# Two DMA queues for the first loads, a first split on VectorE and another order of the first products in a one-core decoder-layer kernel

## Chip, core and metric

The kernel runs on one NeuronCore of one Trainium2 chip. The metric is device microseconds of one execution; a kernel's time is the median over its runs. The engines are called as in the profile: PE (TensorE matmul), PEld (its weight loads), DVE (VectorE), ACT (ScalarE), POOL (GpSimd) and SP (SyncE, which here only issues DMAs).

## What is computed

One decoder layer over 256 tokens of width 1024, all in float32. The change lies in its very first part, the input projection, so this is what matters of the reference:

```python
xn = rms_norm(x, attn_norm_g[l])          # x * rsqrt(mean(x*x) + eps) * g
proj = xn @ w_in[l]                       # 1024 x 3600: mq mk mv gq gk gv gr gate
...
x = x + concat[y_moba, y_gla] @ w_out[l]
x = x + (silu(h_gate) * h_val) @ w_ffn_down[l]
return rms_norm(x, final_norm_g)
```

## The kernel before

**Products in two parts.** Every float32 product a·b is made of three fp32r products: each operand is split into a high part (an fp32r copy) and a low part (the rest), and hi·hi, hi·lo and lo·hi are summed in PSUM (`mm3`, lines 109 to 111). The high part of a weight piece is an ACT activation (`Slot.split_hi`, line 92), the low part a DVE subtraction (`split_lo`, line 95). The input x is split in the same way by `xsplit(k)`: ACT multiplies the tile by the norm's gain and rounds (`ah`, line 169), DVE makes the rest (`al`, line 170). The RMS factor itself is applied later, on the projections' outputs.

**Tiles.** x lies transposed as `xg`: 8 columns of gains and 8 tiles of 128x256 (k = 0 to 7, over the 1024 inputs). The weights come in slots, through a ring of 4 raw buffers and 3 pairs of split buffers. The first four slots hold the group G (gq, the 16 gate columns and gk: 528 columns), two k-tiles to a slot; slot s has `in_wG` of k = 2s and 2s+1. The next ten hold the five other groups of 512 columns (`in_w`), half a group each.

**Order of the work.** PE's order is written out by hand: 64 steps q, in each of which `emit(q)` first does what `plan` holds for q, then the products of that step. Steps 0 to 7 are G's k = 0 to 7 (12 products each: two token halves, columns 0 to 272 into an `acc` bank and 272 to 528 into an `att` bank, three products each). Step 8 begins with `xnorm`: two tiny matmuls of `s1`, the sum over k of x squared, with a column of ones (line 248), before the products of the next group. What makes `s1` is `xsq` (ACT, line 234, two tiles at a time), three `xadd` (DVE, line 237) and `xsum` (DVE, line 241). The order on ACT and DVE is left to a scheduler, which lays it out from its own estimate of times.

**The start.** SP issues all DMAs, in the order of the code: x's tile 0, the first 272 columns of slot 0, the next 256, x's tile 1, the other half of slot 0, x's tile 2, half of slot 1, x's tile 3, the other half, and from there pairs of x tiles and whole slots (lines 147 to 166). ACT loads its function table first (line 54). Six small matmuls of zeros (`warm`, line 73) keep PE at work meanwhile.

Of the kernel before, what the change touches and what calls it, by code (L numbers as in the profile page):

```python
# [9 lines left out]
F32 = mybir.dt.float32  # L10
# [7 lines left out]
KT = 8  # L18
# [8 lines left out]
NG = 256 + RANK + 256  # L27
# [7 lines left out]
def trunk_kernel(ctx: ExitStack, tc: tile.TileContext, xT_d, wG_d, w5_d, wo_d, up_d, dn_d,  # L35
                 par_d, gla_g_d, fin_g_d, wgu_d, cos_d, sin_d, causal_d, lvl_d, ident_d, out_d):
    nc = tc.nc
    V, A, T, DMA = nc.vector, nc.scalar, nc.tensor, nc.sync
# [3 lines left out]
    ring = ctx.enter_context(tc.tile_pool(name="ring", bufs=1))  # L42
# [4 lines left out]
    def acc():  # L47
        return ps_acc.tile([128, 512], F32, name="acc")

    def att():  # L50
        return ps_att.tile([128, 512], F32, name="att")


    A.preload_act_table_set("natural_log_exp_and_others")
    par = const.tile([128, NPAR], F32, name="par")
    cos = const.tile([128, S], F32, name="cos")
    sin = const.tile([128, S], F32, name="sin")
# [18 lines left out]
    RAW, SPL = 4, 3  # L76
# [31 lines left out]
    def mm3(out, sh, sl, mh, ml, first, last, **kw):  # L108
        T.matmul(out, sh, mh, start=first, stop=False, **kw)  # L109
        T.matmul(out, sh, ml, start=False, stop=False, **kw)  # L110
        T.matmul(out, sl, mh, start=False, stop=last, **kw)  # L111

    slots = []
# [16 lines left out]
    nload = [0]  # L130

    def load_next():
        if nload[0] < len(items):
            items[nload[0]].load()
            nload[0] += 1


    xg = main.tile([128, KT + KT * S], F32, name="xg")
    pag = xg[:, :KT]
    xT = xg[:, KT:].rearrange("p (k t) -> p k t", k=KT)  # L140
    ah = main.tile([128, KT, S], F32R, name="ah", tag="ah")
    al = main.tile([128, KT, S], F32R, name="al", tag="al")
# [2 lines left out]
    rsx = main.tile([128, 8], F32, name="rsx")  # L145

    slots[0].raw = ring.tile([128, 2048], F32, name="raw", bufs=RAW)
    def load_x(k0, k1):
        a, b = (KT + S * k0 if k0 else 0), KT + S * k1
        DMA.dma_start(xg[:, a:b], xT_d[:, a:b])  # L150

    load_x(0, 1)
    for a, b in ((0, 272), (272, NG), (NG, 2 * NG)):
        DMA.dma_start(slots[0].raw[:, a:b], slots[0].src[:, a:b])
        if b == NG:
            load_x(1, 2)
    nload[0] = 1
    load_x(2, 3)
    slots[1].raw = ring.tile([128, 2048], F32, name="raw", bufs=RAW)
    DMA.dma_start(slots[1].raw[:, :NG], slots[1].src[:, :NG])  # L160
    load_x(3, 4)
    DMA.dma_start(slots[1].raw[:, NG:2 * NG], slots[1].src[:, NG:])
    nload[0] = 2
    for s in range(2, 4):
        load_x(2 * s, 2 * s + 2)
        load_next()

    def xsplit(k):
        A.activation(ah[:, k], xT[:, k], AF.Copy, scale=pag[:, k:k + 1])
        V.scalar_tensor_tensor(al[:, k], xT[:, k], pag[:, k:k + 1], ah[:, k],  # L170
                               op0=ALU.mult, op1=ALU.subtract)
# [59 lines left out]
    st = {}  # L231
# [305 lines left out]
    def on(q, f, *a):  # L537
        plan.setdefault(q, []).append((f, a))

    for k in range(1, KT):  # L540
        on(k - 1, xsplit, k)
    for dst, src, q in ((ident, ident_d, 1), (par, par_d, 3), (wgu, wgu_d, 4), (cos, cos_d, 4),
                        (sin, sin_d, 4), (lvl, lvl_d, 10), (causal, causal_d, 14), (glag, gla_g_d, 24)):
# [20 lines left out]
    for l in range(7):  # L564
        b = 21 + 11 * l // 4
# [13 lines left out]
    for h in range(HM):  # L579
        b = 30 + 3 * h // 2  # L580
# [13 lines left out]
    for n, sl in enumerate(slots[1:], 1):  # L594
# [5 lines left out]
        on(qa, sl.split, 0, sl.n // 2)  # L600
        on(qa + (3 if q0 - qa > 4 else 1), sl.split, sl.n // 2, sl.n)

    slots[0].alloc()
    xsplit(0)
    for a, b in ((0, 272), (272, NG), (NG, 2 * NG)):
        slots[0].split(a, b)

    def emit(q):
        for f, a in plan.get(q, []):
            f(*a)  # L610

    names = ["G", "q", "k", "v", "gv", "r"]
    for q in range(48):
        g, k = divmod(q, 8)
        emit(q)
        if k == 0:
            if g == 0:
                st["G"] = [(acc(), att()) for _ in range(2)]
            else:
                st[names[g]] = [acc() for _ in range(2)]  # L620
        if g == 0:
            h_, l_ = slots[k // 2].view(NG)
            kk = k % 2
        else:
            h_, l_ = slots[4 + 2 * (g - 1) + k // 4].view(512)
            kk = k % 4
        if g in (1, 2):
            for pr in range(4):
                cs = slice(pr * 128, pr * 128 + 128)
                mm3(st[names[g]][pr // 2][:, (pr % 2) * S:(pr % 2 + 1) * S], h_[:, kk, cs], l_[:, kk, cs],  # L630
                    ah[:, k], al[:, k], k == 0 and pr % 2 == 0, k == KT - 1, skip_group_check=True)
            continue
        for tt in range(2):
            sh = ah[:, k, tt * 128:(tt + 1) * 128]
            sl = al[:, k, tt * 128:(tt + 1) * 128]
            if g == 0:
                a, b = st["G"][tt]
                parts = ((a[:, :272], 0, 272), (b[:, :256], 272, 528))
            else:
                parts = ((st[names[g]][tt], 0, 512),)  # L640
            for o, c0, c1 in parts:
                mm3(o, sh, sl, h_[:, kk, c0:c1], l_[:, kk, c0:c1], k == 0, k == KT - 1)
# [6 lines left out]
    for q in range(48, 64):  # L649
# [5 lines left out]
        h_, l_ = slots[14 + 2 * ph + j // 4].view(512)  # L655
        cs = slice((j % 4) * 128, (j % 4 + 1) * 128)
        for kk in range(4):
            k = 4 * ph + kk
# [281 lines left out]
    for tt in range(2):  # L940
        y = yy[:, tt]
        c = 12 * tt
# [87 lines left out]
```

## Time and profile before

| | before |
|---|---|
| median of 3 runs | 317.51 us (316.83 to 317.53) |
| the profiled execution | 317.25 us, of it a span of 315.4 us from first to last instruction |
| PE, DVE, ACT busy | 97%, 80%, 65% of the span |
| DMA, in slices of 7.9 us | 184, 385, 414, 413, 202 GB/s, then between 0 and 418 |
| granted TensorE clock over the span | 0.999 of full speed |

The busy share of PE counts a modelled end of each matmul, so a stretch that reads as all busy has no long gap, but is not PE at its peak. A row of the timeline gives start, duration, engine, line, what is written and read, the count of instructions that were merged, and in brackets the idle time of the engine before it with what ended it. Instructions of one engine overlap by a little, so the step from one start to the next is the price of one in a row of them.

### The profile page before, as it was taken

Reading aid. Unit: us, or ns where it says so; the run is one execution under the profiler, and the core shown is the slowest. Engines: PE = TensorE matmul, PEld = TensorE weight load, DVE = VectorE, ACT = ScalarE, POOL = GpSimd, SP = SyncE. Lnnn points to the kernel's source line nnn. Section 1 sums busy time; section 2 is a strip of 40 time slices with the busy share of each in tenths; the row PEclk is TensorE's granted clock in tenths of the full one; section 3 lists DMA queues with packets and bytes.
Section 4 is the critical chain, followed back from the end, with each engine's and each line's share of the span. In section 5 each row is a group of like instructions: output and inputs, shape, how many; then the busy total and the mean of one; then the engine's idle time right before and its main releaser. Section 6 shows DMA issues by size and latency. Waiting matters only on the chain.

```text
span 315.4 us, 5842 instructions
## 1 busy us (share of the span) xinstructions
PE 305.8 (97%) x2296; PEld 282.5 (90%) x2296; DVE 253.5 (80%) x478; ACT 203.7 (65%) x370; POOL 3.9 (1%) x17
## 2 busy tenths in 40 slices
PE   6999999999999999999999999999999999999992
PEld 5899997776888999999999999999999999999982
DVE  3987999999647577999999978887777777776653
ACT  5978989497858478366776555666665555534353
POOL 4000000000000000000000000000000000000000
PEclk9999999999999999999999999999999999999999
DMA  6999533342360515595555664454555722120003
GB/s 184 385 414 413 202 135 133 133 151 118 135 232 37 189 79 199 165 418 221 199 202 204 232 220 176 182 197 193 201 202 199 264 70 69 66 69 0 2 0 134
DMA packets 12300, 55.39 MB, mean 176 GB/s; under 512 B 1377, under 2 KB 2929, under 8 KB 7921
## 3 DMA queue, kind: packets, MB, share of 16 engines
q1 hardware_dynamic: 12272, 55.02, 47.3%
q8 instruction: 18, 0.29, 0.4%
q14 instruction: 10, 0.07, 0.1%
HBM read 53.97 MB, written 1.05 MB: 174 GB/s over the span
## 4 chain that ended last, share of the span: by engine, by line
PE 79%; DVE 10%; ACT 5%; issue 2%; DMA 2%; SPq 1%; DVEq 0%; ACTq 0%
PE att L110 14%; PE att L111 14%; PE att L109 14%; PE acc L110 11%; PE acc L109 10%; PE acc L111 10%; DVE lo L95 2%; DMA xg<-in_xT 2%; ACT qs L466 1%; DVE qt L351 1%; DVE att L495 1%; PE att L527 1%; DVE ATd L377 1%; DVE kt L345 1%; PE att L515 1%
## 5 line engine op out<-in xcount | busy, mean ns | idle before, releaser
L92 ACT ACTIVATE hi<-raw 128x1024 fp32r<-128x1024 f32 (+3 forms) x84 | 80.1, 971 | 51.0 <-PE att L110 43.2
L95 DVE TENSOR_TENSOR lo<-raw,hi 128x1024 fp32r<-128x1024 f32 (+3 forms) x86 | 93.6, 1098 | 13.5 <-ACT hi L92 13.4
L109 PE MATMUL att<-hh,hi 128*128 128x256 f32 x352 | 98.5, 280 | 0.0
L111 PE MATMUL att<-hh,lo 128*128 128x256 f32 x352 | 98.4, 279 | 0.0
L110 PE MATMUL att<-hl,hi 128*128 128x256 f32 x352 | 98.3, 279 | 0.0
L109 PEld LDWEIGHTS att<-hh,hi 128*128 128x128 f32 x352 | 66.2, 188 | 0.0
L111 PEld LDWEIGHTS att<-hh,lo 128*128 128x128 f32 x352 | 66.2, 188 | 0.0
L110 PEld LDWEIGHTS att<-hl,hi 128*128 128x128 f32 x352 | 66.2, 188 | 0.0
L757 DVE SCALAR_TENSOR_TENSOR c<-us,par,c 128x256 f32<-128x256 f32 x88 | 40.7, 482 | 4.1 <-ACT c L749 2.5
L749 ACT ACTIVATE c<-us,par 128x256 f32<-128x256 f32 x44 | 24.0, 591 | 21.5 <-DVE us L739 16.1
L111 PE MATMUL acc<-dhi,gl 128*128 128x512 f32 (+1 forms) x88 | 32.3, 367 | 0.0
L110 PE MATMUL acc<-dlo,gh 128*128 128x512 f32 (+1 forms) x88 | 32.2, 366 | 0.0
L109 PE MATMUL acc<-dhi,gh 128*128 128x512 f32 (+1 forms) x88 | 31.8, 361 | 0.0
L696 DVE TENSOR_TENSOR dlo<-draw,dhi 128x1024 fp32r<-128x1024 f32 x22 | 26.6, 1219 | 0.0
L739 DVE TENSOR_TENSOR us<-att,rb 128x512 f32<-128x512 f32 x20 | 13.8, 689 | 15.9 <-PE att L111 15.9
L109 PE MATMUL acc<-hi,ah 128*128 128x512 f32 (+1 forms) x64 | 25.2, 394 | 1.2 <-ACT hi L92 1.2
L110 PE MATMUL acc<-lo,ah 128*128 128x512 f32 (+1 forms) x64 | 24.1, 376 | 0.8 <-DVE lo L95 0.8
L111 PE MATMUL acc<-hi,al 128*128 128x512 f32 (+1 forms) x64 | 23.6, 368 | 0.0
L691 ACT ACTIVATE dhi<-draw 128x1024 fp32r<-128x1024 f32 x22 | 23.1, 1049 | 0.0
L110 PEld LDWEIGHTS acc<-dlo,gh 128*128 128x128 f32 x88 | 16.5, 188 | 3.0
L109 PEld LDWEIGHTS acc<-dhi,gh 128*128 128x128 f32 x88 | 16.6, 188 | 2.9
L111 PEld LDWEIGHTS acc<-dhi,gl 128*128 128x128 f32 x88 | 16.5, 188 | 2.6
(192 smaller groups left out, 528.6 us busy)
## 6 DMA issues: line engine op xcount, KB each, us to landing
raw<-in_up SPq DMA_DIRECT2D x22, 1024.0 KB, 4.8
draw<-in_dn SPq DMA_DIRECT2D x22, 512.0 KB, 5.7
raw<-in_w SPq DMA_DIRECT2D x8, 1024.0 KB, 7.3
raw<-in_wo SPq DMA_DIRECT2D x4, 1024.0 KB, 4.8
raw<-in_w SPq DMA_DIRECT2D x4, 512.0 KB, 7.2
raw<-in_wG SPq DMA_DIRECT2D x2, 528.0 KB, 7.0
out_y<-yy SPq DMA_DIRECT2D x4, 256.0 KB, 2.2
raw<-in_wG SPq DMA_DIRECT2D x3, 264.0 KB, 4.7
```

What stands on the lines that cost most here:

```text
L92: A.activation(self.hi[:, a:b], self.raw[:, a:b], AF.Copy)
L95: V.tensor_sub(self.lo[:, a:b], self.raw[:, a:b], self.hi[:, a:b])
L109: T.matmul(out, sh, mh, start=first, stop=False, **kw)
L110: T.matmul(out, sh, ml, start=False, stop=False, **kw)
L111: T.matmul(out, sl, mh, start=False, stop=last, **kw)
L345: V.tensor_mul(blk(kt)[:, :, 0, :], blk(gk_)[:, :, 0, :], blk(e)[:, :, 0, :])
L351: V.tensor_mul(o, q_, e_)
L691: A.activation(hi, downs[i][0], AF.Copy)
L696: V.tensor_sub(lo, d, hi)
L739: V.tensor_tensor(u[:, :, 2:], upo[i][2].rearrange("p (a t) -> p a t", a=2), rb[:, None, :].to_broadcast([128, 2, S]), op=ALU.mult)
L749: A.activation(cv[i][:, a], u[:, a, 2:], AF.Identity, bias=par[:, P_CB + m:P_CB + m + 1], scale=par[:, P_CW + 2 * 2 * NP + m:P_CW + 2 * 2 ...
L757: V.scalar_tensor_tensor(c[:, a], u[:, a, w:w + S], par[:, wc:wc + 1], c[:, a], op0=ALU.mult, op1=ALU.add)
```

## The change

Four things are done at the start of the program.

- x's tiles 0, 1 and 2 with 3 are now three DMAs on ACT's own queue, ahead of ACT's table load; SP's queue begins with slot 0's three pieces. Slot 1 is now one DMA of 1056 columns in place of two halves, and x's tiles 4 to 7 come between the later slots as before.
- The high part of slot 0's first 272 columns is a DVE copy in place of an ACT activation.
- The splits of slot 0 and of x's tiles 0 and 1 are written in another order (`xsplit(1)` now stands ahead of the plan).
- Step 0's twelve products no longer go through `mm3`: they run as hi·ah and hi·al of the first columns, hi·ah and hi·al of the others, then both lo·ah.

```diff
-    A.preload_act_table_set("natural_log_exp_and_others")
...
-    def load_x(k0, k1):
+    def load_x(q, k0, k1):
...
-        DMA.dma_start(xg[:, a:b], xT_d[:, a:b])
-
-    load_x(0, 1)
+        q.dma_start(xg[:, a:b], xT_d[:, a:b])
...
+    with tc.manual_schedule(engines={mybir.EngineType.Activation}):
+        load_x(A, 0, 1)
+        load_x(A, 1, 2)
+        load_x(A, 2, 4)
+        A.preload_act_table_set("natural_log_exp_and_others")
     for a, b in ((0, 272), (272, NG), (NG, 2 * NG)):
         DMA.dma_start(slots[0].raw[:, a:b], slots[0].src[:, a:b])
-        if b == NG:
-            load_x(1, 2)
     nload[0] = 1
-    load_x(2, 3)
-    slots[1].raw = ring.tile([128, 2048], F32, name="raw", bufs=RAW)
-    DMA.dma_start(slots[1].raw[:, :NG], slots[1].src[:, :NG])
-    load_x(3, 4)
-    DMA.dma_start(slots[1].raw[:, NG:2 * NG], slots[1].src[:, NG:])
-    nload[0] = 2
-    for s in range(2, 4):
-        load_x(2 * s, 2 * s + 2)
-        load_next()
+    load_next()
+    load_x(DMA, 4, 6)
+    load_next()
+    load_x(DMA, 6, 8)
+    load_next()
...
-    for k in range(1, KT):
+    for k in range(2, KT):
         on(k - 1, xsplit, k)
...
     slots[0].alloc()
+    V.tensor_copy(slots[0].hi[:, :272], slots[0].raw[:, :272])
     xsplit(0)
-    for a, b in ((0, 272), (272, NG), (NG, 2 * NG)):
-        slots[0].split(a, b)
+    slots[0].split_hi(272, NG)
+    slots[0].split_lo(0, 272)
+    slots[0].split_lo(272, NG)
+    xsplit(1)
+    slots[0].split(NG, 2 * NG)
...
+        if q == 0:
+
+            for mov, sta, c in ((h_, ah, 0), (h_, al, 0), (h_, ah, 1), (h_, al, 1), (l_, ah, 0), (l_, ah, 1)):
+                c0, c1 = ((0, 272), (272, 528))[c]
+                for tt in range(2):
+                    T.matmul(st["G"][tt][c][:, :c1 - c0], sta[:, 0, tt * 128:(tt + 1) * 128], mov[:, 0, c0:c1],
+                             start=mov is h_ and sta is ah, stop=False)
             continue
```

The scheduler lays out ACT and DVE anew, which moves instructions beyond those that the diff names. On DVE, from the first piece of slot 1 (`lo` of 128x528, needed by step 2) to what follows the sum of squares `s`, the order before was:

```order
L95 TENSOR_TENSOR lo<-raw,hi 128x528
L170 SCALAR_TENSOR_TENSOR al<-xg,ah 128x256
L237 TENSOR_TENSOR xsqs<-xsqs 128x512
L95 TENSOR_TENSOR lo<-raw,hi 128x528
L170 SCALAR_TENSOR_TENSOR al<-xg,ah 128x256 x2
L237 TENSOR_TENSOR xsqs<-xsqs 128x512
L95 TENSOR_TENSOR lo<-raw,hi 128x528 x2
L170 SCALAR_TENSOR_TENSOR al<-xg,ah 128x256 x2
L237 TENSOR_TENSOR xsqs<-xsqs 128x512
L95 TENSOR_TENSOR lo<-raw,hi 128x528 x2
L241 TENSOR_TENSOR s_325<-xsqs 128x256
L95 TENSOR_TENSOR lo<-raw,hi 128x1024
```

And the same stretch in the changed kernel, with two lines less in the numbers of the lines:

```order
L94 TENSOR_TENSOR lo<-raw,hi 128x528 x2
L168 SCALAR_TENSOR_TENSOR al<-xg,ah 128x256 x2
L235 TENSOR_TENSOR xsqs<-xsqs 128x512
L94 TENSOR_TENSOR lo<-raw,hi 128x528 x2
L168 SCALAR_TENSOR_TENSOR al<-xg,ah 128x256 x2
L235 TENSOR_TENSOR xsqs<-xsqs 128x512
L94 TENSOR_TENSOR lo<-raw,hi 128x528 x2
L168 SCALAR_TENSOR_TENSOR al<-xg,ah 128x256
L94 TENSOR_TENSOR lo<-raw,hi 128x1024
L235 TENSOR_TENSOR xsqs<-xsqs 128x512
L94 TENSOR_TENSOR lo<-raw,hi 128x1024
L239 TENSOR_TENSOR s_326<-xsqs 128x256
```

The sum `s`, which stood ahead of both 128x1024 pieces (the halves of the first `in_w` slot), now stands behind them, and so does the last addition of squares behind the first of them.

At the head of ACT's order, from the table load to the first piece of slot 1, there stood before:

```order
L54 ACT_TABLE_LOAD
L169 ACTIVATE ah<-xg 128x256
L92 ACTIVATE hi<-raw 128x272
L92 ACTIVATE hi<-raw 128x256
L169 ACTIVATE ah<-xg 128x256
L234 ACTIVATE xsqs<-xg 128x512
L92 ACTIVATE hi<-raw 128x528
L169 ACTIVATE ah<-xg 128x256
L92 ACTIVATE hi<-raw 128x528
```

and now there stands:

```order
L149 DMA xg<-in_xT 128x264
L149 DMA xg<-in_xT 128x256
L149 DMA xg<-in_xT 128x512
L156 ACT_TABLE_LOAD
L167 ACTIVATE ah<-xg 128x256
L91 ACTIVATE hi<-raw 128x256
L167 ACTIVATE ah<-xg 128x256
L91 ACTIVATE hi<-raw 128x528
L167 ACTIVATE ah<-xg 128x256
L232 ACTIVATE xsqs<-xg 128x512
L91 ACTIVATE hi<-raw 128x528 x2
```

Three DMA issues come ahead of the table load, one split has left for DVE, and the first squares moved behind the half of slot 0 and x's tile 2, just ahead of slot 1's two pieces.

## Rows read from the trace of the kernel before

**Rows 1.** The page: busy time by engine, and the chain that ended last.
```profile
PE 305.8 (97%) x2296; PEld 282.5 (90%) x2296; DVE 253.5 (80%) x478; ACT 203.7 (65%) x370; POOL 3.9 (1%) x17
...
PE 79%; DVE 10%; ACT 5%; issue 2%; DMA 2%; SPq 1%; DVEq 0%; ACTq 0%
```

**Rows 2.** The waits of PE, whole span: us in total, times, longest us.
```profile
PE acc L109 <- ACT hi L92: 1.2, 2, 0.9
...
PE acc L110 <- DVE lo L95: 0.8, 3, 0.4
PE att L527 <- ACT pe L500: 0.6, 1, 0.6
```

**Rows 3.** Timeline of PE: first product, two of one row of them, the sum's matmuls.
```profile
4.32 0.39 PE L109 MATMUL acc<-hi,ah 128*128 128x272 f32 x1 [0.35 <-ACT hi L92]
...
13.69 0.29 PE L111 MATMUL acc<-hi,al 128*128 128x272 f32 x1
...
15.51 0.28 PE L111 MATMUL att<-hi,al 128*128 128x256 f32 x1
...
19.28 0.50 PE L248 MATMUL att<-ones,s 128*128 128x1 f32 x4
```

**Rows 4.** Timeline of ACT to its first piece of slot 1.
```profile
0.73 1.28 ACT L54 ACT_TABLE_LOAD   x1 [0.73 <-PEq L1019]
3.44 0.51 ACT L169 ACTIVATE ah<-xg 128x256 fp32r<-128x256 f32 x1 [1.43 <-DMA xg<-in_xT]
...
6.13 0.61 ACT L234 ACTIVATE xsqs<-xg 128x512 f32<-128x512 f32 x1
6.65 0.63 ACT L92 ACTIVATE hi<-raw 128x528 fp32r<-128x528 f32 x1
7.18 0.49 ACT L169 ACTIVATE ah<-xg 128x256 fp32r<-128x256 f32 x1
8.26 0.65 ACT L92 ACTIVATE hi<-raw 128x528 fp32r<-128x528 f32 x1 [0.58 <-DMA raw<-in_wG]
```

**Rows 5.** Timeline of SP: its first DMA issues.
```profile
0.73 0.37 SPq L150 DMA_DIRECT2D xg<-in_xT  x1
1.16 0.89 SPq L154 DMA_DIRECT2D raw<-in_wG  x2
2.10 0.43 SPq L150 DMA_DIRECT2D xg<-in_xT  x1
```

**Rows 6.** Windows: busy us of PE, PEld, DVE, ACT, POOL; PEclk; DMA share, GB/s.
```profile
0.00:2.00 2.00, 0.95 (x4) 0.95 (x5) 0.17 (x1) 1.27 (x1) 1.47 (x10) 1.00 0.10 20
2.00:4.00 2.00, 1.97 (x10) 1.68 (x8) 0.02 (x1) 0.57 (x3) 1.94 (x5) 1.00 0.89 226
4.00:6.00 2.00, 1.52 (x10) 1.31 (x11) 1.16 (x3) 0.86 (x3) 0.35 (x1) 1.00 0.88 274
6.00:8.00 2.00, 0.86 (x5) 0.45 (x4) 1.17 (x3) 1.68 (x4) 0.00 (x0) 1.00 0.87 214
8.00:10.00 2.00, 1.93 (x14) 1.81 (x15) 1.48 (x4) 1.63 (x4) 0.00 (x0) 1.00 0.96 321
...
12.00:14.00 2.00, 1.71 (x14) 1.50 (x13) 2.00 (x5) 2.00 (x6) 0.00 (x0) 1.00 1.01 415
```

**Rows 7.** Timeline of DVE, from slot 1's first low part on.
```profile
8.94 0.71 DVE L95 TENSOR_TENSOR lo<-raw,hi 128x528 fp32r<-128x528 f32 x1 [0.52 <-ACT hi L92]
...
12.70 1.32 DVE L95 TENSOR_TENSOR lo<-raw,hi 128x528 fp32r<-128x528 f32 x2
13.94 0.87 DVE L170 SCALAR_TENSOR_TENSOR al<-xg,ah 128x256 fp32r<-128x256 f32 x2
14.73 0.68 DVE L237 TENSOR_TENSOR xsqs<-xsqs 128x512 f32<-128x512 f32 x1
15.34 1.32 DVE L95 TENSOR_TENSOR lo<-raw,hi 128x528 fp32r<-128x528 f32 x2
16.57 0.42 DVE L241 TENSOR_TENSOR s<-xsqs 128x256 f32<-128x256 f32 x1
16.91 1.22 DVE L95 TENSOR_TENSOR lo<-raw,hi 128x1024 fp32r<-128x1024 f32 x1
18.05 0.21 DVE L286 TENSOR_TENSOR id<-ident 128x64 f32<-128x64 f32 x1
```

More of the change, by code (lines that the diff above doesn't have):

```diff
@@ L631, in trunk_kernel @@
                     ah[:, k], al[:, k], k == 0 and pr % 2 == 0, k == KT - 1, skip_group_check=True)
+            continue
+        if q == 0:
[4 more added lines that the diff above has]
+                             start=mov is h_ and sta is ah, stop=False)
             continue
```

## The prediction

> **What bounds the kernel now.** I read the page first: PE is busy for 97% of the span and carries 79% of the chain that ended last [rows 1]. A kernel like this gets faster only where PE stands still, so the second view is PE's waits [rows 2]: 1.2 us for high parts, 0.8 us for low parts, both in the first steps, and one wait of 0.6 us in the attention (line 527). The start is therefore the place to look, and the timeline of PE [rows 3] gives its frame: first product at 4.32, and line 248, the first work behind group G, at 19.28. Without waits the 96 products of G would take 96 x 0.121 = 11.6 us, where 0.121 is (15.51 - 13.69) / 15 starts in an undisturbed piece of it [rows 3]. They took 15.0, so 3.3 us are lost between 4.32 and 19.28, and behind that PE loses almost nothing. Whatever the change gives must show as an earlier line 248, and later waits may eat it.
>
> Who is late there? ACT's timeline [rows 4] shows two kinds of idle time: for x's tiles and for slot 1's first half, which landed just before 8.26. The windows [rows 6] show the DMA engines 0.87 to 0.89 busy from 2 to 8 us but moving only 214 to 274 GB/s, against 415 later. From 8.94 on it is DVE that has no gap: each of its rows begins where the last one stepped off, up to the sum of squares `s` at 16.57 [rows 7], and 12:14 reads 2.00 of 2.00 [rows 6].
>
> **The change part by part.** I count from the profiled execution (317.25 us, 0.26 under the median of 317.51) and add the difference to the median.
>
> *The first step.* SP starts one DMA every 0.47 us (0.73, 1.16, the third at 2.10 behind two merged ones) [rows 5]. With two queues x's tile 0 and slot 0's first piece start together at 0.73. ACT now issues three DMAs first, by SP's price 3 x 0.43 = 1.3 us, so its table load (1.28 us, [rows 4]) ends at 3.3 instead of 2.0; the first tile of x was there at 3.44. That hides it, by little. The DVE copy of 272 columns has no row of its own; it lies between 0.21 (128x64) and 0.71 (128x528) [rows 7], and I take 0.4, as it is nearer in size to half a 128x528. First product at about 4.1. DVE makes lo ahead of al, so the order hi·al before lo cannot be met quite as written; still the twelve products are over by 6.0. Step 1 needs the second half of slot 0, which (below) is not split before 6.9. So the copy, the new order of products and the earlier first product are all worth nothing by themselves: the next step is late next, and if an ACT issue cost twice SP's, this too would be covered.
>
> *The loads up to slot 1.* Before, slot 1's first half landed at 8.24, with 132 + 136 + 128 + 128 + 264 + 128 + 264 = 1180 KB of 1024 bytes up to it in SP's queue, 1.21 MB. By the windows [rows 6] 2 x (20 + 226 + 274 + 214) = 1468 thousand bytes had moved by 8.0 and 1545 by 8.24, so 0.34 MB of later pieces were under way. Now slot 1 comes whole: 132 + 136 + 128 + 128 + 264 + 256 + 528 = 1572 KB, 1.61 MB, and with the same 0.34 MB under way 1.95 MB have to move, 1.91 of them from 2.0 on. Three prices: at 415 GB/s (the full rate) it lands at 6.6; at the rates of before, window by window, at 9.5; at 321 GB/s, the rate of 8:10, at 7.9. I take the last, because from 8 us on several DMAs of 2 to 4 KB rows stood ready, which with two queues holds from the start. By the same count the half of slot 0 and x's tiles 2 and 3 (1.07 MB, 1.37 to move from 2.0) land at 5.3, 7.7 and 6.3. Behind them ACT has a split (0.53 from 6.65 to 7.18), one x tile (at most 0.51) and the squares (0.52) [rows 4], 1.5 us, and is free at 6.8, 9.2 and 7.8. ACT's first piece of slot 1 so starts at 6.8, 9.5 and, taken, 8.0; before it was 8.26.
>
> *What DVE then has to do before line 248.* This is the part that the diff does not show. The sum `s` used to be ready at 17.0, 2.3 us before PE asked for it. Now the scheduler puts both halves of the first `in_w` slot ahead of it. From the first low part of slot 1 there are six of 128x528 at 0.62, five of x at 0.40, three additions at 0.61, two pieces of 128x1024 at 1.14 and `s` at 0.42 (steps between starts, [rows 7]): 3.72 + 2.00 + 1.83 + 2.28 + 0.42 = 10.25 us. They start 0.66 us after ACT's piece (0.65 in [rows 4]). PE needs less: from that low part (0.71) on, 71 products at 0.121, 9.3 us. So **DVE is 0.9 us later than PE and line 248 gets a wait that it did not have**; it starts 0.66 + 10.25 + 0.05 = 10.96 us after ACT's first piece of slot 1, at 18.96 with 8.0. That is 19.28 - 18.96 = 0.3 us earlier than before. ACT's own list for the same stretch is shorter, and the loads behind slot 1 move at the full rate, so I charge them nothing; if they were late, it would be the second `in_w` half that DVE waits for.
>
> *Behind line 248.* The same orders of DVE and ACT hang on it, so it carries the gain on. The scheduler has exchanged neighbours up to about 75 us, and the wait of line 527 (0.58 us of idle time) can go or grow; I take 0, with 0.4 either way, two thirds of that wait. SP has fewer issues and the same bytes.
>
> Sum: 0.3 us less, 317.25 - 0.3 = 316.95 for the profiled kind of run, **317.2 us** as a median. A measurement of this kernel can tell about 0.3%, 0.95 us, from no change, so this would read as the same.
>
> **Rivals.**
>
> *The loads run full from the start (faster).* If starved DMA engines are all that holds the first 8 us, two queues take 415 GB/s at once: ACT's piece starts at 6.8, line 248 at 17.8, and the gain is 1.5 us, 316.0. It decides at a start before 7.4 (8.32 - 0.95). For it: SP's 0.47 us for 128 KB is 280 GB/s, an issue limit under the full rate. Against it: at a step of 0.47 us SP had some ten DMAs out by 5.5, and still the rate from 4 to 8 was 274 and then 214 at 0.87 to 0.88 busy [rows 6], so issue was not the whole cause.
>
> *Slot 1 comes as late as its bytes (slower).* At the rates of before, the whole slot 1 lands at 9.5 and not in two halves from 8.24; DVE's 10.25 us start 1.2 us later than before with the longer list ahead of `s`, line 248 slips to 20.5 and the kernel takes 318.7. It decides at a start of ACT's piece after 9.3. For it: the engines already read 0.87 to 0.89 busy with one queue [rows 6], and x's tiles now share them with the pieces that step 1 needs. The Trainium skill says the same in DMA: Bandwidth & Descriptors, section Issuing engines are not separate DMA queues: DMAs issued by several engines run on the same 16 DMA engines, and a second issuer saves only issue time. By that rule nothing but the 0.47 us steps is won and this rival's 318.7 would be the time; the busy shares of 0.87 to 0.89 agree with it, while the low GB/s at that share speak for slack that better-filled queues could use.
>
> *The wait at line 248 does not come.* If DVE gets through its list without PE noticing (the copy and fewer gaps make it start earlier than I count), PE's 9.3 us decide and the gain is 0.9 us more than the sum, 316.3. For that DVE's step prices would have to fall, and [rows 7] hold them steady; I give it little.
>
> **How the numbers follow.** Forecast, 0.3 us less: 0.57; its own range, with the start of ACT's piece from 7.4 to 9.2, is 316.6 to 318.4. Loads at full rate, 316.0: 0.24. Slot 1 late, 318.7: 0.13. No wait at line 248, 316.3: 0.04. What happens in the attention, 0.4 us either way, is in all of them; 0.02 is left for something slower that I do not see. Faster by over 0.3%: 0.24 + 0.04 = 0.28; within: 0.57; slower: 0.13 + 0.02 = 0.15. For 8 times in 10 the range reaches the faster case's middle and most of the way to the slower one: 315.9 to 318.4.
>
> **What would show it.** Right: slot 1's split starting near 8.0 on ACT, DVE with no gap from there to `s`, and PE idle for 0.5 to 1.0 us at line 248 with DVE's `s` named as what ended it. The first product near 4.1 and yet step 1 waiting for the half of slot 0 until about 7 would show that the first step is worth nothing. Wrong: no wait at line 248; the split of slot 1 before 7.4 or after 9.3; or a shift of line 248 that the end of the span does not repeat, which would put the answer into the attention.

## The result, and the profile after

The changed kernel takes 318.86 us, the median of six runs (318.58 to 319.67); the kernel before, run beside it, 317.30. The ratio is 1.0057, with a 95% interval of 1.0046 to 1.0067. That is 1.6 us slower, outside the range of the prediction and on the other side of its forecast. The profiled execution took 318.75, with a span of 317.0 against 315.4.

PE is still busy for the same share. The page of the changed kernel:

```profile
PE 308.2 (97%) x2296; PEld 285.1 (90%) x2296; DVE 254.0 (80%) x479; ACT 203.0 (64%) x369; POOL 4.0 (1%) x17
```

Its busy time has grown by 2.4 us [rows 1] with the same 2296 instructions, so some of them ran longer. The waits of PE (us in total, times, longest) look better than before [rows 2]: those for high and low parts are off the list. But a new one of 0.6 us stands there, at line 268, the transposes of the gate columns:

```profile
PE att L268 <- ACT gqk L262: 0.6, 1, 0.6
...
PE att L525 <- ACT pe L498: 0.4, 1, 0.4
```

PE's timeline tells the rest. Line 246 is the old 248, the sum's matmuls; 268 is the old 270.

```profile
4.43 0.82 PE L641 MATMUL acc<-hi,ah 128*128 128x272 f32 x2 [0.45 <-ACT ah L167]
...
9.74 0.43 PE L108 MATMUL acc<-hi,ah 128*128 128x272 f32 x1
9.97 0.43 PE L109 MATMUL acc<-lo,ah 128*128 128x272 f32 x1
...
11.74 0.41 PE L108 MATMUL att<-hi,ah 128*128 128x256 f32 x1
11.96 0.36 PE L109 MATMUL att<-lo,ah 128*128 128x256 f32 x1
12.16 0.28 PE L110 MATMUL att<-hi,al 128*128 128x256 f32 x1
12.28 0.28 PE L108 MATMUL acc<-hi,ah 128*128 128x272 f32 x1
...
20.30 0.50 PE L246 MATMUL att<-ones,s 128*128 128x1 f32 x4
...
24.00 0.27 PE L268 MATMUL att<-ident,gqk 128*16 128x128 f32 x1
24.87 0.28 PE L268 MATMUL att<-ident,gqk 128*16 128x128 f32 x1 [0.60 <-ACT gqk L262]
```

The same places in the kernel before:

```profile
5.10 0.29 PE L111 MATMUL acc<-hi,al 128*128 128x272 f32 x1
5.23 0.28 PE L109 MATMUL att<-hi,ah 128*128 128x256 f32 x1
...
22.97 0.38 PE L270 MATMUL att<-ident,gqk 128*16 128x128 f32 x2
```

Read the steps between starts. Until 12.16 one product of 272 columns follows the other after 0.23 us, which is 1.2 GHz (272 columns in 0.227 us are 1.2 per ns); from there after 0.12, which is 2.4 GHz [rows 3]. In the kernel before, the short step was there from 5 us on. The trace's record of the granted clock says the same: it begins at 12.13 with full speed, and in the kernel before at 3.93. What lies ahead of its first entry is counted as full, so the PEclk column of the windows reads 1.00 there and does not show the slow stretch. The sum's matmuls start 1.0 us later than before (20.30 against 19.28), with no wait in front of them. The second transpose starts 4.57 us after them; before, the two stood 3.8 apart. So 0.8 more is lost there, and the attention gives 0.2 back: 1.0 + 0.8 - 0.2 = 1.6, the difference of the spans. The 0.2 is the wait in the attention, 0.4 at line 525 where 0.6 stood at line 527 [rows 2].

ACT's timeline shows both ends of this, the first splits and the evacuations of G (lines 262, 263):

```profile
3.87 0.51 ACT L167 ACTIVATE ah<-xg 128x256 fp32r<-128x256 f32 x1 [0.46 <-DMA xg<-in_xT]
...
7.04 0.64 ACT L91 ACTIVATE hi<-raw 128x528 fp32r<-128x528 f32 x1 [1.20 <-DMA raw<-in_wG]
7.59 0.49 ACT L167 ACTIVATE ah<-xg 128x256 fp32r<-128x256 f32 x1
7.99 0.61 ACT L232 ACTIVATE xsqs<-xg 128x512 f32<-128x512 f32 x1
8.51 1.16 ACT L91 ACTIVATE hi<-raw 128x528 fp32r<-128x528 f32 x2
...
22.64 0.49 ACT L262 ACTIVATE gqk<-acc,rsx 128x272 f32<-128x272 f32 x1 [1.05 <-DVE rsx L179]
23.03 0.47 ACT L263 ACTIVATE gqk<-att,rsx 128x256 f32<-128x256 f32 x1
23.38 1.05 ACT L91 ACTIVATE hi<-raw 128x1024 fp32r<-128x1024 f32 x1
24.33 0.49 ACT L262 ACTIVATE gqk<-acc,rsx 128x272 f32<-128x272 f32 x1
```

ACT waited for slot 0's third piece until 7.04; before, ACT started that split at 6.65 without a wait [rows 4]. And a high part of 1.05 us now stands between the two token halves' evacuations, for which the second transpose waits. DVE, from slot 1's first low part:

```profile
9.17 1.33 DVE L94 TENSOR_TENSOR lo<-raw,hi 128x528 fp32r<-128x528 f32 x2 [0.35 <-ACT hi L91]
...
16.07 1.22 DVE L94 TENSOR_TENSOR lo<-raw,hi 128x1024 fp32r<-128x1024 f32 x1
17.21 0.68 DVE L235 TENSOR_TENSOR xsqs<-xsqs 128x512 f32<-128x512 f32 x1
17.81 1.22 DVE L94 TENSOR_TENSOR lo<-raw,hi 128x1024 fp32r<-128x1024 f32 x1
18.94 0.42 DVE L239 TENSOR_TENSOR s<-xsqs 128x256 f32<-128x256 f32 x1
```

Its list up to the end of `s` took 19.36 - 9.17 = 10.2 us, as predicted (10.25); it only began late. The windows (the last number is GB/s):

```profile
2.00:4.00 2.00, 1.98 (x10) 1.68 (x8) 0.30 (x1) 1.42 (x2) 1.94 (x5) 1.00 0.87 224
4.00:6.00 2.00, 1.57 (x6) 1.50 (x7) 1.38 (x4) 1.19 (x3) 0.46 (x1) 1.00 0.95 298
6.00:8.00 2.00, 1.87 (x9) 1.57 (x7) 0.65 (x2) 0.96 (x3) 0.00 (x0) 1.00 1.01 393
8.00:10.00 2.00, 1.85 (x8) 1.54 (x9) 1.65 (x4) 2.00 (x6) 0.00 (x0) 1.00 1.03 409
```

Until 6 us they are nearly those of before (226 and 274), and then 393 and 409 where 214 and 321 stood [rows 6]. In this kernel the two queues move more bytes, but only after the time in which the first pieces are needed.

### The profile page after: what moved, and what is told of

It is laid out like the page before. It is cut to its first block, busy times and chain, and to the rows that moved or that the text cites. A ratio compares the mean times of both kernels' runs of the same rounds, so it can differ in the third digit from the quotient of the medians.

```text
span 317.0 us, 5839 instructions
## 1 busy us (share of the span) xinstructions
PE 308.2 (97%) x2296; PEld 285.1 (90%) x2296; DVE 254.0 (80%) x479; ACT 203.0 (64%) x369; POOL 4.0 (1%) x17
## 3 DMA queue, kind: packets, MB, share of 16 engines
HBM read 53.97 MB, written 1.05 MB: 174 GB/s over the span
## 4 chain that ended last, share of the span: by engine, by line
PE 84%; DVE 9%; ACT 2%; DMA 2%; issue 1%; SPq 0%; DVEq 0%; ACTq 0%
PE att L108 14%; PE att L109 14%; PE att L110 14%; PE acc L109 12%; PE acc L108 12%; PE acc L110 12%; DVE lo L94 3%; DMA raw<-in_wG 2%; DVE qt L349 1%; DVE att L493 1%; PE att L525 1%; DVE kt L343 1%; DVE ATd L375 1%; PE att L513 1%; ACT pe L498 1%
## 5 line engine op out<-in xcount | busy, mean ns | idle before, releaser
L94 DVE TENSOR_TENSOR lo<-raw,hi 128x1024 fp32r<-128x1024 f32 (+3 forms) x86 | 93.7, 1098 | 15.9 <-ACT hi L91 15.8
```

The source lines that it names most:

```text
L94: V.tensor_sub(self.lo[:, a:b], self.raw[:, a:b], self.hi[:, a:b])
```

## The experiments

The three suspects are the loads (third piece of slot 0 late, so DVE's list late), the clock (1.2 GHz until 12 us), and the order on ACT (a split between the evacuations). The table sums up what the runs gave. "1.2 GHz until" is where the trace's record of the granted clock begins with full speed in the profiled execution; a value under 4.6 lies ahead of the first product. "Sum" is where line 246 or its counterpart starts there.

| kernel | loads | orders | 1.2 GHz until | sum | median, us |
|---|---|---|---|---|---|
| before | old | old | 3.9 | 19.28 | 317.2 to 317.3 |
| before, 4 small matmuls | old | old | 8.2 | 19.1 | 317.31 |
| orders alone | old | new | 9.2 | 19.94 | 318.07 |
| loads alone | new | new | 12.8 | 20.9 | 319.29 |
| changed | new | new | 12.1 | 20.30 | 318.86 |
| changed, again | new | new | 12.9 | 20.74 | 319.58 |
| changed, 9 small matmuls | new | new | 7.2 | 20.46 | 319.06 |
| evacuations together | new | `s` late | 13.4 | 21.1 | 318.61 |
| the same, 8 small matmuls | new | `s` late | 7.0 | 20.70 | 317.98 |
| the same, 9 small matmuls | new | `s` late | 4.3 | 19.78 | 317.79 |
| x's tiles 2, 3 on SP | mixed | old | 4.5 | 18.9 | 317.46 |
| old loads, rest changed | old | old | 9.7 | 19.5 | 316.70 (again: 316.98) |

The table can be checked against the times. The profiled execution's time less the start of the sum's matmuls is 297.7 to 298.0 us in the kernel before and in the eleven other profiles with the evacuations side by side and the x loads of either kernel; it is 298.35 to 298.48 in the three with x's tiles 0 and 1 alone on ACT's queue, and 298.45 to 299.24 in the five with a split between the evacuations. So what is lost up to the sum reaches the end of the program, and the split costs 0.5 to 1.3 us behind it.

**The clock, the split, and both.**

```diff
-WARM = 6
+WARM = 9
```

> The changed kernel with nine small matmuls of zeros at the start in place of six (each runs 0.43 us as two of 0.21), so that they end at about 5.0 instead of 3.77. Clock theory: in the changed kernel G's products start every 0.21 to 0.23 us until 12.16 (the level of 1.2 GHz) and 0.12 behind it; with PE at work up to the first product the step falls to 0.12 before 6 us, the first sum matmul (line 246) starts at about 19.4, when DVE's s is done, instead of 20.30, and the median is 318.0 (0.9 less than 318.86). DVE theory (the list ahead of s holds PE, whatever the clock): line 246 stays between 20.0 and 20.4 and the time at 318.6 to 318.9. Bytes theory (slot 1 late): also no gain, and 0 to 0.6 lost to the later first product (5.05).

```diff
-        A.activation(gqk[:, tt, 0:272], a[:, :272], AF.Copy, scale=rstd(tt))
-        A.activation(gqk[:, tt, 272:528], b[:, :256], AF.Copy, scale=rstd(tt))
+        with tc.high_priority():
+            A.activation(gqk[:, tt, 0:272], a[:, :272], AF.Copy, scale=rstd(tt))
+            A.activation(gqk[:, tt, 272:528], b[:, :256], AF.Copy, scale=rstd(tt))
```

> The changed kernel with the scheduler told to put the four evacuations of G (lines 262, 263) ahead of other ACT work, so that the high part of a 128x1024 piece no longer stands between the two token halves. Split theory: the wait of 0.60 us at the transposes of the gate columns (line 268) goes, 0.7 less: 318.1 to 318.3, with the step of the first products still 0.21 to 0.23 until about 12 and line 246 at 20.3. Rival (the wait only moves to the next consumer of the piece that is now split later): a wait of 0.4 to 0.6 on a high part of line 91 behind 25 us and 318.7 to 318.9.

> Both edits together. If the late rise of the clock (0.9) and the split between the evacuations (0.7) are two causes that add up, 317.2 to 317.4, equal to the kernel before. If they hide each other (PE earlier at line 246 then waits longer at line 268 or behind it), 317.9 to 318.3.

Nine matmuls alone gave 319.06 (ratio 1.0059, 1.0047 to 1.0071), no gain. The clock was up at 7.2, but slot 0's third piece came only at 7.99 in that execution, `s` ended at 20.31, and the wait at the transposes grew to 1.0. The evacuations alone gave 318.61 (1.0046, 1.0033 to 1.0058): the wait at the transposes (now line 269) is gone, but the gain of 0.25 is within the intervals, and in its profile slot 0's third piece was split at 7.50 in place of 7.04. Both together gave 317.79 (1.0023, 1.0012 to 1.0034): 1.1 us better than the changed kernel, neither the sum nor the hiding that I expected. What is left of the loss, 0.6, stands as a wait in that kernel's list:

```profile
PE att L246 <- DVE id L285: 0.7, 1, 0.7
```

(The row names the instruction behind `s`; the matmuls start 0.14 us after the end of `s`, here and in the run with the orders alone, where nothing follows it.)

```diff
-WARM = 6
+WARM = 4
```

> The kernel before with four small matmuls in place of six, which end at about 2.9, so that PE stands still for 1.4 us ahead of its first product (4.32) instead of 0.5. Clock theory: the step of the first products is 0.21 to 0.23 for several us, as in the changed kernel; here slot 1's halves and all orders are those of before, so what the low level alone costs shows: line 248 at 19.9 to 20.4 instead of 19.28, and 318.0 to 318.4. Rival (the warm-up does not matter, PE is held by the loads and splits in this stretch anyway): line 248 within 0.2 of 19.28, 317.2 to 317.5.

With four small matmuls the kernel before took 317.31 (1.0004, 0.9995 to 1.0012): no loss. Its products took 0.22 until 8.2:

```profile
7.75 0.43 PE L111 MATMUL acc<-hi,al 128*128 128x272 f32 x1
7.98 0.39 PE L109 MATMUL att<-hi,ah 128*128 128x256 f32 x1
8.19 0.29 PE L110 MATMUL att<-lo,ah 128*128 128x256 f32 x1
```

So the clock theory is wrong as I put it: here a low level until 8 us is free, since PE would otherwise stand and wait for the next pieces. Only a later rise can cost. With the evacuations alone, where it came at 13.4, it did: there `s` ended at 20.01 and the sum's matmuls started only at 21.1.

**The loads.** First the old loads with all else of the change (the lines on `load_x`, `load_next` and the table load undone), then the new loads with nothing else of it (those lines alone), then one DMA moved back.

> The changed kernel with the loads and the table load of the kernel before (all on SP, slot 1 in halves); the first high part on VectorE, the order of the splits and the order of the first products stay as changed. The scheduler's orders of DVE and ACT from slot 1 on are then those of before. Theory (all that is lost comes from the loads and from the orders that follow them): 317.0 to 317.4, no wait at the transposes, no wait for s. Rival (the copy on VectorE or the order of the first products costs as well): 317.8 or more, seen as a later half of slot 0 or a slower step 0.

> The kernel before with the new loads alone (three x DMAs and then the table load on ACT, slot 1 whole); high parts, splits and products as before. The scheduler again puts s behind both 128x1024 pieces and a split between the two token halves' evacuations. Theory (loads and orders are the cause): 318.4 to 319.2, with the wait of 0.5 to 1.0 at the transposes and the sum matmuls at 19.8 or later. Rival (it takes all parts together): 317.2 to 317.6.

```diff
-        load_x(A, 2, 4)
...
     nload[0] = 1
+    load_x(DMA, 2, 4)
     load_next()
```

> The changed kernel with one DMA moved: x's tiles 2 and 3 go back to SP's queue, behind slot 0's third piece and ahead of slot 1; x's tiles 0 and 1 stay on ACT's queue. With this the scheduler puts s ahead of both 128x1024 pieces and the four evacuations side by side, as before. Theory (third piece of slot 0 shares the engines with x's tiles 2 and 3, and the orders do the rest): that piece's split starts before 7.0, no wait at the transposes, line 246 at 18.8 to 19.5, 316.8 to 317.4. Rival (two queues as such, or the whole slot 1, make it late): the split still at 7.0 to 8.0 and 317.8 or more.

The old loads gave 316.70 (0.9988, 0.9979 to 0.9996), the loads alone 319.29 (1.0066, 1.0053 to 1.0079), and the moved DMA 317.46 (1.0012, 1.0003 to 1.0021), a little above what I expected. All that the change loses comes with its loads and the orders that follow from them. Moving the one DMA of x's tiles 2 and 3 back to SP's queue takes 1.4 us of it away (318.86 to 317.46). In that profile slot 0's third piece is split at 6.19 in place of 7.04, the clock is up at 4.5, and the orders are those of before; the run does not part these three.

**DVE's list ahead of `s`.**

```diff
+            first = (f == xsplit or f in (xadd, xsum, xsq) or f in [s.split for s in slots[:4]])
+            with tc.high_priority(offset=50) if first and q > 1 else ExitStack():
```

> As the run with nine small matmuls and the evacuations together, and besides the splits of x and of slots 1 to 3, the squares and s are given a little more weight in the scheduler (an offset of 50), so that s stands ahead of the second 128x1024 piece on DVE instead of behind it: 1.14 us less ahead of s. Theory (DVE's list ahead of s holds line 246): the wait of 0.7 there goes, the time falls by 0.5 to 0.8 to 317.0 to 317.3. Rival (PE is held by the loads and the 1.2 GHz level; s is only named last): no gain, 317.6 to 318.0.

This gave 319.92 (1.0088, 1.0073 to 1.0103), and is no test of the list: the weight also moved the splits of x's tiles 2 and 3 ahead of slot 0's third piece on ACT, and they had to wait for a DMA. PE stood for 0.7 and then 1.5 us, and its clock, already up, fell back:

```profile
7.06 0.39 PE L644 MATMUL att<-hi,al 128*128 128x256 f32 x2
7.29 0.41 PE L644 MATMUL acc<-lo,ah 128*128 128x272 f32 x2
...
9.48 0.60 PE L108 MATMUL acc<-hi,ah 128*128 128x272 f32 x1 [1.54 <-ACT hi L91]
...
10.61 0.43 PE L110 MATMUL acc<-hi,al 128*128 128x272 f32 x1
10.84 0.41 PE L108 MATMUL att<-hi,ah 128*128 128x256 f32 x1
```

The step was 0.12 before the stand, and 0.23 behind it (10.61 to 10.84) until 15.8; the granted clock reads 1.00 from 5 to 9 us, 0.50 from 9 to 15.8 and 1.00 again behind. `s` ended at 19.98, the sum's matmuls started at 23.0. A cleaner cut leaves every order as it is:

```diff
-        V.tensor_add(xsqs[:, 0:2], xsqs[:, 0:2], xsqs[:, 2 * n:2 * n + 2])
+        (V if n == 3 else nc.gpsimd).tensor_add(xsqs[:, 0:2], xsqs[:, 0:2], xsqs[:, 2 * n:2 * n + 2])
```

> The kernel with nine small matmuls and the evacuations together (317.79, wait of 0.7 at line 246), and besides the first two additions of squares on GpSimd instead of VectorE; all orders stay, DVE has 2 x 0.61 = 1.2 us less ahead of s. Theory (DVE's list ahead of s holds line 246 once the clock is up): the wait of 0.7 at line 246 is gone or under 0.2 and the time is 317.0 to 317.3. Rival (DVE is only named, PE cannot go earlier for the loads, or the additions on GpSimd hold DVE): no gain, 317.6 to 318.2.

It gave 318.65 (1.0052, 1.0032 to 1.0071), 0.86 slower than without it. DVE with nine small matmuls and the evacuations together:

```profile
12.08 1.32 DVE L94 TENSOR_TENSOR lo<-raw,hi 128x528 fp32r<-128x528 f32 x2
13.32 0.87 DVE L168 SCALAR_TENSOR_TENSOR al<-xg,ah 128x256 fp32r<-128x256 f32 x2
14.11 0.68 DVE L235 TENSOR_TENSOR xsqs<-xsqs 128x512 f32<-128x512 f32 x1
...
19.22 0.42 DVE L239 TENSOR_TENSOR s<-xsqs 128x256 f32<-128x256 f32 x1
```

and with the additions on GpSimd (POOL):

```profile
11.70 2.08 DVE L94 TENSOR_TENSOR lo<-raw,hi 128x528 fp32r<-128x528 f32 x2 [0.27 <-ACT hi L91]
13.70 1.94 DVE L168 SCALAR_TENSOR_TENSOR al<-xg,ah 128x256 fp32r<-128x256 f32 x2
15.56 1.32 DVE L94 TENSOR_TENSOR lo<-raw,hi 128x528 fp32r<-128x528 f32 x2
...
20.07 0.41 DVE L239 TENSOR_TENSOR s<-xsqs 128x256 f32<-128x256 f32 x1
```

```profile
11.29 1.30 POOL L235 TENSOR_TENSOR xsqs<-xsqs 128x512 f32<-128x512 f32 x1 [6.94 <-ACT xsqs L232]
13.67 1.28 POOL L235 TENSOR_TENSOR xsqs<-xsqs 128x512 f32<-128x512 f32 x1 [1.08 <-ACT xsqs L232]
```

Beside each addition DVE takes longer: 2.00 in place of 1.24 us for two low parts of 128x528, 1.86 in place of 0.79 for two of x. Taken singly, it is the first of each pair, the one that runs beside the addition (1.46 in place of 0.70 us, 1.54 in place of 0.48); the second low part took 0.70 as ever. Together that is more than the two additions would have cost. So the cut became a lengthening, and as such it answers the question: `s` ended 0.84 later (20.48 against 19.64), the sum's matmuls started 0.84 later (20.62 against 19.78), and the kernel was 0.86 slower. With the clock up, DVE's list sets that time one for one.

**The orders alone.** In the kernel before, both new orders are written by hand.

```diff
...
+        with tc.manual_schedule(engines={mybir.EngineType.DVE}):
+            slots[4].split(1024, 2048)
+            xsum()
...
+        with tc.manual_schedule(engines={mybir.EngineType.Activation}):
+            g_evac(0)
+            slots[6].split(0, 1024)
+            g_evac(1)
...
```

> The kernel before with its own loads and products, in which only the two orders of the changed kernel are written by hand: s behind both 128x1024 pieces on DVE, and a 128x1024 high part between the evacuations of the two token halves on ACT. Theory: s comes 2 x 1.14 later, at 18.85 to 19.3, just in time for line 248 (0 to 0.1 lost), and the split between the evacuations costs 0.6 to 0.8 at the transposes: 317.8 to 318.1. Rival (the orders cost only together with late loads): 317.2 to 317.4. If the orders were all of the change's loss: 318.7.

318.07 (1.0030, 1.0018 to 1.0042): 0.9 us, as the theory said, so the orders are about half of the change's loss and not all of it. In the profiled execution (319.18, the slowest of its twelve) the sum's matmuls start at 19.94, 0.14 behind the end of `s`, and the wait at the transposes is 1.3, of which 0.58 is ACT's wait for the load of the piece in between. The profile of the changed kernel does not have that wait, so some of the 0.9 may be it. The rows:

```profile
22.75 0.47 ACT L265 ACTIVATE gqk<-att,rsx 128x256 f32<-128x256 f32 x1
23.80 1.06 ACT L92 ACTIVATE hi<-raw 128x1024 fp32r<-128x1024 f32 x1 [0.58 <-DMA raw<-in_w]
24.76 0.47 ACT L264 ACTIVATE gqk<-acc,rsx 128x272 f32<-128x272 f32 x1
```

**The clock once more, and tries at a faster kernel.** The first of these is the kernel with the old loads and six small matmuls again, for another profile.

> The run with the old loads once more, for a profile of another execution: its profiled one took 317.25 with the first products at 0.22 us until 9.7, while the median of its eleven runs is 316.70. If the level of the clock makes that difference, an execution near 316.7 shows the step of the products at 0.12 before 8 and line 248 at 18.7 to 19.0; if not, the same 0.22 until past 9.

> The changed kernel with the evacuations together and eight small matmuls, which end at about 4.4, where the first product starts. Clock theory: an early rise as with nine (317.79, against 318.61 with six) but no later start: 317.6 to 317.8, line 246 held by s alone at 19.6 to 19.9. Rival (it was not the clock but the luck of the landings that parted 317.79 from 318.61): 318.4 to 318.8.

> The old loads with the changed copy, splits and first products (316.70 with six) and eight small matmuls. Clock theory: no execution with a late rise is left, 316.3 to 316.6 and a smaller spread. Rival: the rise depends on later standing (5.7 to 7.3, when PE waits for slot 0's third piece, as in the second profile of that kernel), so nothing changes: 316.6 to 316.9, same spread.

The single further execution with the old loads took 317.55: its products ran at 0.12 from 4.7, then at 0.22 from 8.1 to 11.5, after PE had stood for 1.3 us waiting for slot 0's third piece. On the changed kernel with the evacuations together, eight matmuls gave 317.98 (1.0030, 1.0020 to 1.0040), between six (318.61) and nine (317.79) and a little above what I expected: by the medians the early rise is worth 0.6 to 0.8 there, though the intervals of six and eight overlap. On the old loads they gave 316.96 (0.9996, 0.9987 to 1.0004), nothing.

```diff
-        load_x(A, 2, 4)
...
-    nload[0] = 1
-    load_next()
+    load_x(DMA, 2, 3)
+    slots[1].raw = ring.tile([128, 2048], F32, name="raw", bufs=RAW)
+    DMA.dma_start(slots[1].raw[:, :NG], slots[1].src[:, :NG])
+    load_x(DMA, 3, 4)
+    DMA.dma_start(slots[1].raw[:, NG:2 * NG], slots[1].src[:, NG:])
+    nload[0] = 2
```

> A try at a version that beats both: the changed kernel, but only x's tiles 0 and 1 on ACT's queue, and SP's queue as before behind slot 0's three pieces (x's tile 2, half of slot 1, tile 3, the other half). The scheduler then keeps the orders of before. By the run with the old loads (316.70) and that with tiles 2 and 3 on SP (317.46, slot 1 whole): 316.5 to 316.9 if the halves of slot 1 are what the latter lacked, 317.3 to 317.6 if two queues at the start bring nothing.

> x's tiles 0 and 1 on ACT's queue and the rest as before on SP's (317.22 with six, from 316.43 to 317.71, the 316.43 with the step of the products at 0.13 from the first on), with eight small matmuls. Clock theory: all executions like the best, 316.3 to 316.7. Rival (something else, as landings, spreads them): 317.0 to 317.3.

> The kernel before with the new order of the first twelve products alone. The prediction gave these edits nothing. Theory now, from the old loads (0.5 faster): hi·al and lo need not come in turn, so PE is freed of the 0.16 and 0.2 us waits in step 0, but step 1 waits for slot 0's third piece: 317.1 to 317.3, no gain. Rival (the gain of the old loads comes from here): 316.6 to 316.9.

With only x's first two tiles on ACT's queue the median was 317.22 (0.9999, 0.9987 to 1.0012; runs from 316.43 to 317.71), with eight matmuls 316.99 (0.9995, 0.9983 to 1.0007; 316.17 to 317.81). Their profiled executions (316.43, the fastest of its twelve, and 316.57) reached the sum's matmuls at 18.1 and 18.2, more than 1 us earlier than before. In them the DMA engines moved 376 and 369 GB/s from 4 to 6 us, where the eight profiles with the old loads have 248 to 300 and the nine with the new loads 262 to 298. With the same two tiles on ACT's queue and slot 1 whole (the moved DMA) it is 293. So a second queue can bring early bytes when only x's first two tiles are on it and slot 1 comes in halves. But the runs spread over more than 1.2 us with six matmuls and with eight; what spreads them stays open. The first products alone gave 317.05 (0.9994, 0.9984 to 1.0004), no gain, as predicted.

> The changed kernel itself, for another profile and more times. If the late rise is its usual course (the two kernels with its loads and six small matmuls, with evacuations together and loads alone, rose at 13.4 and 12.8): the step of the products 0.21 to 0.23 until 11 to 14 us, line 246 at 20.1 to 21.2, 318.6 to 319.1. If the rise of the first profile was luck: a rise before 9, line 246 at s's end (19.4 to 19.9) and a wait of 0.8 or more at the transposes, at about the same time, since that wait takes back what the clock gives (as with nine small matmuls).

> The old loads with the rest of the change, again. If the gain of the first time is real: 316.6 to 317.0, ratio at most 0.999. If not: 317.0 to 317.3.

The changed kernel took 319.58 this time (1.0070, 1.0057 to 1.0083), more than I expected. Its clock rose at 12.9, so the late rise is the usual course: with these loads and six small matmuls, four profiles of four show it at 12.1 to 13.4. But here `s` ended only at 20.59, and the sum's matmuls followed it (20.74). PE started the last of its products at 20.55 and was free for the next at 20.67, so in this execution a faster PE would have gained nothing at that place, and an earlier `s` alone less than 0.1. ACT shows why `s` was so late:

```profile
7.04 0.64 ACT L91 ACTIVATE hi<-raw 128x528 fp32r<-128x528 f32 x1 [0.98 <-DMA raw<-in_wG]
8.81 0.51 ACT L167 ACTIVATE ah<-xg 128x256 fp32r<-128x256 f32 x1 [1.13 <-DMA xg<-in_xT]
9.22 0.61 ACT L232 ACTIVATE xsqs<-xg 128x512 f32<-128x512 f32 x1
9.74 0.63 ACT L91 ACTIVATE hi<-raw 128x528 fp32r<-128x528 f32 x1
```

Here x's tiles 2 and 3 were the late ones. The old loads with the rest of the change gave 316.98 (0.9992, 0.9983 to 1.0001): at best 0.1% under the kernel before. No version beat both by more than a measurement can tell.

## Why the prediction was wrong

**Right.** The first step's edits are worth nothing or little (317.05 for the new order alone, 316.70 and 316.98 for all of them with the old loads; the first product came at 4.43, not 4.1, for x's tile 0 landed at 3.87). DVE's list of 10.25 us took 10.2. With an early clock the sum's matmuls do get the predicted wait, 0.7 where I said 0.9. The attention gave 0.2, inside its 0.4.

**Wrong, first: "I take the last", 321 GB/s from 2.0 on.** By it the third piece of slot 0 was there at 6.3, ACT free at 7.8 and slot 1's first split at 8.0. The windows had 224 and 298 until 6 and 393 behind. With these, my own count puts the third piece at 6.8 (1.37 MB, of which 1.04 by 6.0 and 0.33 at 393) and slot 1 at 8.2; ACT started on them at 7.04 and 8.51. So the bytes ahead were counted about right and the rate from 2 to 6 us was not. In eight of the nine profiles with these loads (the ninth has another order on ACT) it began the third piece at 7.0 to 8.0 and slot 1 at 8.5 to 9.7; with the old loads it began the third piece at 5.9 to 6.7 in eight profiles. The Trainium skill says in DMA: Bandwidth & Descriptors, section Issuing engines are not separate DMA queues, that DMAs of all issuers run on the same engines and interleave. Up to 6 us the windows of this kernel agree with it. With x's first two tiles alone on ACT's queue and slot 1 in halves the 376 and 369 GB/s from 4 to 6 are more than two saved steps of issue (0.47 us each) would give, since the kernel before had 306 at most in any microsecond from 4 to 7. How much of the 393 behind 6 us is the second queue and how much the larger DMA of slot 1 is not shown. I had put this down to the rival "slot 1 comes as late as its bytes", with a chance of 0.13; its 318.7 is near what was measured, but in good part by luck: ACT's piece started on both sides of its 9.3 (8.51 in the profile that took 318.75), and more than half of the loss lies elsewhere.

**Wrong, second: "PE needs less: from that low part (0.71) on, 71 products at 0.121, 9.3 us".** Until 12.16 PE paid 0.22 apiece. From 8.87 on that is 15 products at 0.22 in place of 0.12, 1.5 us; without it PE would have been at the sum at 18.8 and waited for `s` until 19.5. So in the profiled execution 0.8 of the 1.0 us at line 246 is the clock and 0.2 the late list. In the later one both were late together (PE free at 20.67, `s` letting it go at 20.74): there either alone would have cost nearly the whole 1.46. Whichever of the two is later sets the time. The list of waits has none at line 246 in either profile, which the prediction had named as a sign of being wrong. Two things turned the level of the clock into a cost here: it rose late, and the pieces came late enough that the products had to run in that stretch. I had read the clock of the kernel before as a given. Why it rises later with these loads is not shown: with the old loads and six small matmuls the record of the granted clock begins at 3.93, 3.95, 4.7, 4.7, 9.2 and 9.7 in six profiles.

**Wrong, third: "The same orders of DVE and ACT hang on it, so it carries the gain on", with a cost of 0 behind line 248.** ACT's new order put a 1.05 us split between the evacuations, and the transposes waited: 0.8 here, 1.2 in the later execution, and 0.9 of loss from the two orders alone with the old loads. This stood in the order of the changed kernel before it ever ran; I had compared it only up to `s`.

In the profiled execution the three add up to the miss. The prediction has line 246 at 18.96. ACT's piece at 8.51 in place of 8.0 makes that 19.5, the clock 20.3; the transposes add 0.8 and the attention takes 0.2 off. Together 0.5 + 0.8 + 0.8 - 0.2 = 1.9 us, from a forecast 0.3 shorter to a span 1.6 longer. Between kernels the parts overlap and do not simply add: 0.9 (orders alone, with the old loads, `s` behind both pieces included), 0.6 (late list: nine matmuls, evacuations together) and 0.6 to 0.8 (late clock) are no breakdown of the 1.6 to 2.4 measured, since the clock costs only where `s` is not later still. How much of each is in the median is not shown.

## What to carry to other kernels

When DMAs are spread over two queues, ask which piece is needed next and what now travels beside it: a higher rate can come with a later first piece. When a scheduler lays out an engine anew, compare its order as far as it differs, not only up to the wait you have in mind; a split that slips between two evacuations can cost most of its length if a matmul waits for both (0.8 of 1.05 us here). And a term that counts PE's products at the full clock holds only if the clock is up in that stretch after the change; work the sum out at the low level too.

## What the runs showed of the hardware

The clock's level at the start differs between executions of one kernel: with the old loads it was up at 9.7 in one profile, at 4.7 and down again from 8.1 to 11.5 in the next, and at 3.95 in the third, with the same matmuls ahead. The Trainium skill, in TensorE: Matmul & The Clock Gate, section What's actually happening, calls the number of slow first matmuls run-variable; these profiles agree.

Two additions of 1.3 us on GpSimd stretched the two DVE instructions beside them by 1.8 us in all (1.46 in place of 0.70, 1.54 in place of 0.48); each ended 0.3 to 0.6 us behind the addition. The Trainium skill, in SBUF — State Buffer, section SBUF: two separate sides, says that VectorE and GpSimd share a pair of ports as an exclusive lock; these rows agree that work moved to GpSimd is not free for VectorE.
